# One step of a gated-linear-attention / gMLP decoder on one core: key halves joined in one row of matmuls, prompt states from fp32r parts, later state updates

## The chip, the cores and the metric

The kernel runs on one core of a Trainium2 chip. Its time is the device time of one execution in microseconds. A run's profile is the record of one execution by the hardware profiler; its span is the time from the first to the last instruction of the program. Engines are named as in the profile: PE multiplies matrices and PEld loads its weights, DVE and ACT do elementwise work, POOL and SP mostly start transfers here.

## The reference

The program computes one inference step of a decoder of two layers for two groups of tokens: a prompt of 256 new tokens, and 8 samples of 8 new tokens each. The model width is 2048.

Layer 0 mixes tokens by gated linear attention. Four heads have keys of 256 and values of 512. For each head a state S of 256 x 512 is carried along:

```
S_t = diag(a_t) S_{t-1} + k_t^T v_t          o_t = q_t S_t
o   = o * rsqrt(mean(o^2) + eps) * norm_g * silu(r)        then   o @ w_out
```

The prompt begins with S = 0 and returns its last state. Each sample brings a state of its own, and its eight tokens read that state and update it; the new state is an output too. q, k, v, r and a low-rank gate all come from one projection of x.

Layer 1 mixes tokens by a gMLP with a causal 128 x 128 matrix for each of eight groups. After each mixer comes `x = LayerNorm(alpha * x + mixer)`, then an MLP, `square(relu(x @ w1)) @ w2` with a hidden width of 8192, and again a LayerNorm of the sum. Everything is fp32.

## The kernel before

Activations lie with features on partitions and the 320 tokens (256 of the prompt, 64 of the samples) in the free dimension. The large products are done in three fp32r matmuls: both the weight and the activation are split into a high part (an fp32r cast) and a low part (the rest), and `mm3` adds low·high, high·low and high·high (L186 to L188). I call these the ordinary matmuls.

A unit of work is a weight tile of 512 rows by 256 columns. `unit` loads it from DRAM on SP's queue into `raw`, ACT casts it to the high part (L168) and DVE subtracts for the low part (L169). PE then does 2 x 4 x 3 = 24 matmuls over 320 columns. `group` walks the four units of a column block (`NU = 4`) and gives the finished PSUM tiles to an `evict` function. After each unit it calls `side`, which runs the next of a list of smaller steps: `Side` spreads its steps evenly over the units that are left, one or more to a unit, and `Spread` does the same with a fixed ratio. This order is that of emission. A scheduler then orders each engine's instructions by an estimated timeline, and may take a step earlier where its data are there.

In layer 0 each head takes 24 units: 8 for values (`project_v`), 8 for keys and queries (`project_kq`), 8 for the output gate r (`project_r`). The head's own attention is a list of steps (`Head.steps`) that runs beside `project_r` of the head and `project_v` of the next. In the last head there is no next `project_v`, and the list gets 10 units in place of 16. The steps that matter here:

- `split(n)`, n = 0 to 7: one quarter-head of two samples' states is brought into three bf16 parts (L632 to L635: cast, subtract, cast, subtract, each over 128 x 1024). The parts lie in four `sp` buffers, and each split starts the load of a later state on SP's queue.
- `sample_first` and `sample_group(kt)`: four samples at a time (`hd.g` is 0, then 1) multiply their queries with their states. `sample_first` is one fp32r matmul over 512 columns with the part within the eight tokens (L642). `sample_group(kt)` takes one half of the key dimension, kt = 0 or 1: three parts times four samples are 12 bf16 matmuls (L651), each with 32 columns of weights, that write the four quarters of one PSUM tile. `sample_out` evicts and transposes it.
- `prompt_scores`, `prompt_o(i)`: attention within the prompt, in fp32.
- `gather_k(q)`: transfers on POOL's queue (SP's in the last head) that finish the transposing of the prompt's decayed keys into `ktp`.
- `prompt_state(kt)`: the prompt's last state for one half of the key, `ktp` times the prompt's values in `va`, in fp32 (L604). It is evicted by ACT (L606) and stored.

In both MLPs the samples' states are updated beside the matmuls: `updates` yields a list of steps for 16 pairs of head and sample. A step `decay` scales a state on ACT, and eight steps `token` add one token's outer product each, two operations on DVE (L915). `paced` ties a step to the newest high part of a weight, so that it cannot run long before its place. `Spread` gives the 161 steps to 216 units. It starts with the third column block of the MLP's first product: the first two are done in raw form by `gemm_of`, while the LayerNorm is still being applied by `Norm.apply` (L853, L854, L856, L857, L859, the last of which writes the low part `yl`). The same `gemm_of` begins the gMLP layer's projection, with no updates beside it.

Of the kernel before, what the change touches and what calls it, by code (L numbers as in the profile page):

```python
# [8 lines left out]
F32 = mybir.dt.float32  # L9
F32R = mybir.dt.float32r  # L10
# [6 lines left out]
P = 128  # L17
D = 2048
KT = D // P
TP = 256  # L20
DB, DS = 8, 8
T = TP + DB * DS
TW = T + 2
H = 4
DK, DV = 256, 512
CH = 64
# [7 lines left out]
NU = KT // UK  # L34
# [62 lines left out]
def step_kernel(ctx: ExitStack, tc: tile.TileContext, A):  # L97
    nc = tc.nc
    uid = [0]

    def nm(s):
        uid[0] += 1
        return f"{s}_{uid[0]}"
# [23 lines left out]
    def gltile(n=512):  # L127
        return gl.tile([P, n], F32, tag="gl", name=nm("gl"), padded_shape=[P, 512])
# [20 lines left out]
    def col(c):  # L149
        return vec[:, c : c + 1]  # L150
# [88 lines left out]
    gp = gst.enter_context(tc.tile_pool(name="gp", bufs=1))  # L239
# [18 lines left out]
    def load_x(q):  # L258
        for i, raw in enumerate(x_in(q)):
            x_parts(slice(4 * q + 2 * i, 4 * q + 2 * i + 2), raw[:, :, 0:T])  # L260
# [10 lines left out]
    nc.vector.memset(smask[:, TP:T:DS], 0.0)  # L271

    W0, W1 = TP, TP - P
    mf = gp.tile([P, DV], F32, tag="kip", name="mf")[:, 0 : W0 + W1]
    nc.gpsimd.memset(mf, 1.0)
    for c0, w in ((0, W0), (W0, W1)):
        nc.gpsimd.affine_select(out=mf[:, c0 : c0 + w], in_=mf[:, c0 : c0 + w], compare_op=ALU.is_ge, fill=0.0,
# [21 lines left out]
    qm = gp.tile([P, 2, DB, 4, DS], BF16, tag="qm", name="qm")  # L299
# [48 lines left out]
    def pairs(t):  # L348

        return t[:].rearrange("p (a v f) -> p a v f", a=2, v=2)  # L350
# [12 lines left out]
    class Head:  # L363
# [5 lines left out]

        def tiles(hd):  # L370
            hd.qd = gp.tile([P, 2, T], F32, tag="qd", name=nm("qd"))
            hd.qx = gp.tile([P, 2, 5 * CH], F32, tag="qx", name=nm("qx"))
            hd.kip = gp.tile([P, 2, TP], F32, tag="kip", name=nm("kip"))
            hd.kte = gp.tile([P, 2, T], F32, tag="kte", name=nm("kte"))
            hd.kis = gp.tile([P, 2, DB, 2, DS], F32, tag="kis", name=nm("kis"))

            hd.ktp = gp.tile([P, 2, 2, P], F32, tag="ktp", name=nm("ktp"))
            hd.va = gp.tile([P, 2, 6, P], F32, tag="vtp", name=nm("va"))

        def vt_prompt(hd, vt, blk):  # L380
            return hd.va[:, vt // 2, vt % 2 * 2 + blk, :]

        def v_prompt(hd, blk):
            return hd.va[:, :, blk : blk + 3 : 2, :]

        def v_sample(hd):
            return hd.va[:, :, 4:6, :].bitcast(F32R)
# [211 lines left out]
        def prompt_state(hd, kt):  # L599
            if kt == 0:  # L600
                hd.S = g3.tile([P, 2, DV], F32, tag="st", name=nm("S"))
            pu = gltile()
            for blk in range(2):
                nc.tensor.matmul(pairs(pu), hd.ktp[:, kt, blk, :], hd.v_prompt(blk),  # L604
                                 start=(blk == 0), stop=(blk == 1))
            nc.scalar.copy(hd.S[:, kt, :], pu[:])  # L606
            if kt == 1:
                nc.gpsimd.dma_start(A["o_state_p"][hd.h].rearrange("(k p) v -> p k v", p=P), hd.S[:])
# [19 lines left out]
        def split(hd, n):  # L628

            s = hd.st.pop(n)  # L630
            hd.sp[n] = sp = g3.tile([P, 3, 2, DV], BF16, tag="sp", name=nm("sp"))
            nc.scalar.copy(sp[:, 0], s[:])  # L632
            nc.vector.tensor_sub(s[:], s[:], sp[:, 0])
            nc.scalar.copy(sp[:, 1], s[:])
            nc.vector.tensor_sub(sp[:, 2], s[:], sp[:, 1])  # L635
            if n + 3 < 8:
                hd.load(n + 3)
# [4 lines left out]
            nc.tensor.matmul(pairs(hd.po), scst[:, hd.g].rearrange("p j c t -> p (j c t)"), hd.v_sample(),  # L642
                             start=True, stop=False)

        def sample_group(hd, kt):

            n = 4 * hd.g + 2 * kt
            sp = [hd.sp.pop(n), hd.sp.pop(n + 1)]
            for c in (2, 1, 0):
                for j in range(4):  # L650
                    nc.tensor.matmul(hd.po[32 * j : 32 * (j + 1), :],  # L651
                                     qm[:, kt, 4 * hd.g + j].rearrange("p c t -> p (c t)"),
                                     sp[j // 2][:, c, j % 2, :], start=False, stop=(kt == 1 and c == 0))

        def sample_out(hd):

# [30 lines left out]
        def steps(hd):  # L687

            def split(n, also=lambda: None):
                return lambda: (also(), hd.split(n))  # L690

            yield hd.sample_scores
            yield hd.prompt_scores
            yield split(2, hd.sample_first)
            yield lambda: hd.prompt_o(0)
            yield lambda: (hd.sample_group(0), hd.gather_k(0))
            yield split(3, lambda: hd.prompt_o(1))
            yield split(4, lambda: hd.gather_k(1))
            yield lambda: (hd.sample_group(1), hd.gather_k(2))
            yield split(5, lambda: (hd.sample_out(), hd.gather_k(3)))  # L700
            yield split(6, hd.sample_first)
            yield lambda: hd.sample_group(0)
            yield split(7)
            yield lambda: hd.prompt_state(0)
            yield lambda: (hd.sample_group(1), hd.prompt_state(1))
            yield hd.sample_out
            yield hd.sums
            yield hd.weigh
            yield hd.finish
# [2 lines left out]
    warm_up()  # L712
    for h, hd in enumerate(hds):
        gates = [hd.gate_logits, hd.gate_sums, hd.gate_decays]
        if h == 0:

            side = Side([lambda: None, lambda: load_x(1), lambda: None, lambda: load_x(2), lambda: load_gates(),
                         lambda: load_x(3), low_gate, *gates], 4 * NU)
            hd.project_v(side)
            for step in (hd.begin_states, lambda: hd.split(0), lambda: hd.split(1)):  # L720
                side.steps.append(step)
            hd.project_kq(side)
        else:
            hd.project_v(side)
            hd.project_kq(Side([hd.begin_states, *gates, lambda: hd.split(0), lambda: hd.split(1)], 2 * NU))
        side = Side(hd.steps(), 2 * NU + (2 * NU if h < H - 1 else 2))
        hd.project_r(side)

# [150 lines left out]
    def updates(todo):  # L879
# [20 lines left out]
        def decay(h, b):  # L900
            st = cur[h, b]
            row(h, b, 0)
            row(h, b, 1)
            d = paced(dec_all[:, h, :, NCH + b])
            for kt in range(2):
                nc.scalar.activation(st[:, kt, :], st[:, kt, :], AF.Identity, scale=d[:, kt : kt + 1])
# [13 lines left out]
        begin(*todo[0])  # L920
        for i, (h, b) in enumerate(todo):
            if i == 0:
                yield lambda: None
                yield lambda: None
            yield lambda h=h, b=b: decay(h, b)
            for t in range(DS):
                yield lambda h=h, b=b, t=t: token(h, b, t)
                if t == 2 and i + 1 < len(todo):
                    yield lambda n=todo[i + 1]: begin(*n)
# [77 lines left out]
    def before(q):  # L1007
        if q == NU - 1:
            second_half()
        else:  # L1010
# [3 lines left out]
                         side=side, before=before)  # L1014
# [101 lines left out]
    for step in "n0 n2 m0 m1 n4 n6 m2 m3 m4 m5 n8 n10 m6 m7 m8 m9 n12 n14 m10 m11 m12 m13 m14 m15".split():  # L1116
        j = int(step[1:])
        steps.append((lambda j=j: mix2(j)) if step[0] == "n" else lambda j=j: mixed(j, *mix(j)))
    side = Side(steps, 6 * NU)
# [47 lines left out]
    for j in range(KT):  # L1167
        y, g, b = z[:, j, :], col(norm.vg + j), col(norm.vb + j)
# [4 lines left out]
        else:  # L1173
            if j not in ps:
                put_d(j)
            t = l2.tile([P, T], F32, tag="t", name=nm("t"), bufs=3)
# [70 lines left out]
```

## Time and profile before

| | us |
|---|---|
| median of 3 runs | 2664.23 |
| lowest and highest | 2663.86, 2664.64 |
| the profiled execution | 2665.18 |
| its span | 2663.4 |

| engine | busy us | share of the span |
|---|---|---|
| PE | 2651.9 | 100% |
| DVE | 1865.1 | 70% |
| ACT | 1330.6 | 50% |
| POOL | 383.0 | 14% |

The granted clock of PE is 1.0 throughout. Layer 0's four heads lie between about 5 and 405 us, the output projection follows, then the first MLP from about 517 us; the second MLP begins at about 1755 us. In the lists of groups a row shows the line, the engine, the operation, tiles written and read, shape and count, then the total busy time, the mean duration of one in ns, and the idle time before. In the timeline a row shows the start, the busy time, and how many instructions of the same kind were joined. A row of waits shows total, number and longest. A row of windows shows the stretch, its length, and for each engine (PE, PEld, DVE, ACT, POOL) its busy time and number of instructions; where it was asked for one line, only the engine of that line.

### The profile page before, as it was taken

The page shows a single profiled execution, that of the slowest core. Times are in us where ns is not written, and L with a number is a line of the kernel's source. Part 1 is how long each engine was busy: PE and PEld are TensorE (multiplying, and loading weights), DVE is VectorE, ACT ScalarE, POOL GpSimd, SP SyncE. Part 2 cuts the span into 40 slices and gives each one's busy share as a digit, 9 for nine tenths or more (in the row PEclk, how much of TensorE's full clock was granted, in tenths as well). Part 3 has the DMA queues.
Part 4 walks back from the last instruction along what each step waited for, and adds up shares of the span by engine and source line. Part 5 has one row for each costly group of instructions (what it writes and reads, how often), then busy time and mean ns, then how long its engine had stood idle before and what let it go on. Part 6 is the DMA issues. An engine that isn't in the chain of part 4 may idle for free.

```text
span 2663.4 us, 46772 instructions
## 1 busy us (share of the span) xinstructions
PE 2651.9 (100%) x18395; PEld 2625.8 (99%) x18395; DVE 1865.1 (70%) x2798; ACT 1330.6 (50%) x2290; POOL 383.0 (14%) x677
## 2 busy tenths in 40 slices
PE   9999999999999999999999999999999999999999
PEld 9999999999999999999999999999999999999998
DVE  7687686896667667667578765788666666666647
ACT  6575574574444345445346544466445444444434
POOL 4334320011111111111001041001111111111000
PEclk9999999999999999999999999999999999999999
DMA  8566566467767767677554454456767777676642
GB/s 262 164 214 197 155 207 235 149 187 227 225 218 219 223 214 230 213 226 216 177 153 159 151 167 149 150 153 215 231 212 225 216 218 228 213 229 212 198 151 95
DMA packets 163597, 524.88 MB, mean 197 GB/s; under 512 B 25520, under 2 KB 34608, under 8 KB 163376
## 3 DMA queue, kind: packets, MB, share of 16 engines
q1 hardware_dynamic: 121440, 408.08, 48.7%
q0 software_dynamic: 41392, 113.15, 14.5%
q8 instruction: 144, 2.36, 0.4%
q14 instruction: 77, 0.63, 0.1%
q10 hardware_dynamic: 544, 0.66, 0.1%
HBM read 493.48 MB, written 22.54 MB: 194 GB/s over the span
## 4 chain that ended last, share of the span: by engine, by line
PE 96%; DVE 2%; ACT 1%; DMA 1%; issue 0%; SPq 0%; ACTq 0%; DVEq 0%
PE mm L186 32%; PE mm L188 31%; PE mm L187 31%; PE gl L604 1%; DVE wl L169 1%; PE gl L651 0%; DMA st<-state 0%; PE gl L1096 0%; PE gl L588 0%; DMA raw<-gla_w_in 0%; ACT z L1180 0%; ACT wh L168 0%; DVE t L854 0%; DVE t L853 0%; DVE yl L859 0%
## 5 line engine op out<-in xcount | busy, mean ns | idle before, releaser
L169 DVE TENSOR_TENSOR wl<-raw,wh 128x1024 fp32r<-128x1024 f32 (+1 forms) x740 | 901.8, 1220 | 686.8 <-ACT wh L168 681.3
L168 ACT CAST wh<-raw 128x1024 fp32r<-128x1024 f32 (+1 forms) x740 | 771.7, 1044 | 1071.3 <-PE mm L188 937.0
L188 PE MATMUL mm<-yh,wh 128*128 128x320 f32 x2624 | 805.4, 307 | 0.0
L186 PE MATMUL mm<-yh,wl 128*128 128x320 f32 x2624 | 804.2, 308 | 0.0
L187 PE MATMUL mm<-yl,wh 128*128 128x320 f32 x2624 | 794.5, 303 | 2.3 <-DVE yl L859 2.3
L186 PE MATMUL mm<-hh,wl 128*128 128x320 f32 x2048 | 630.8, 308 | 0.0
L188 PE MATMUL mm<-hh,wh 128*128 128x320 f32 x2048 | 628.7, 307 | 0.0
L187 PE MATMUL mm<-hl,wh 128*128 128x320 f32 x2048 | 619.6, 303 | 0.0
L187 PEld LDWEIGHTS mm<-yl,wh 128*128 128x128 f32 x2624 | 492.5, 188 | 2.9 <-DVE yl L859 2.9
L186 PEld LDWEIGHTS mm<-yh,wl 128*128 128x128 f32 x2624 | 491.4, 188 | 0.0
L188 PEld LDWEIGHTS mm<-yh,wh 128*128 128x128 f32 x2624 | 490.8, 187 | 0.0
L187 PEld LDWEIGHTS mm<-hl,wh 128*128 128x128 f32 x2048 | 384.5, 188 | 0.0
L186 PEld LDWEIGHTS mm<-hh,wl 128*128 128x128 f32 x2048 | 384.4, 188 | 0.0
L188 PEld LDWEIGHTS mm<-hh,wh 128*128 128x128 f32 x2048 | 383.0, 187 | 0.0
L915 DVE SCALAR_TENSOR_TENSOR su<-vr,pace,su 128x512 f32<-128x512 f32 x512 | 363.8, 748 | 0.0
L886 POOL DMA_DIRECT2D vr<-v_dram x256 | 139.1, 544 | 1320.3 <-DVE su L915 1282.9
L186 PE MATMUL mm<-xh,wl 128*128 128x320 f32 x768 | 241.2, 316 | 1.5 <-DVE wl L169 1.0
L188 PE MATMUL mm<-xh,wh 128*128 128x320 f32 x768 | 236.7, 309 | 0.0
L187 PE MATMUL mm<-xl,wh 128*128 128x320 f32 x768 | 233.4, 304 | 0.0
L186 PEld LDWEIGHTS mm<-xh,wl 128*128 128x128 f32 x768 | 144.1, 188 | 8.6 <-issue 5.9
L187 PEld LDWEIGHTS mm<-xl,wh 128*128 128x128 f32 x768 | 144.2, 188 | 2.5 <-issue 1.7
L188 PEld LDWEIGHTS mm<-xh,wh 128*128 128x128 f32 x768 | 143.7, 187 | 0.2
(269 smaller groups left out, 2470.1 us busy)
## 6 DMA issues: line engine op xcount, KB each, us to landing
raw<-mlp_w SPq DMA_DIRECT2D x512, 512.0 KB, 4.0
vr<-v_dram POOLq DMA_DIRECT2D x256, 256.0 KB, 4.3
raw<-gla_w_in SPq DMA_DIRECT2D x94, 512.0 KB, 3.9
raw<-sg_w_in SPq DMA_DIRECT2D x64, 512.0 KB, 3.5
st<-state SPq DMA_DIRECT2D x32, 512.0 KB, 5.1
raw<-gla_w_out SPq DMA_DIRECT2D x32, 512.0 KB, 4.3
su<-state POOLq DMA_DIRECT2D x32, 512.0 KB, 6.8
o_state_s<-su POOLq DMA_DIRECT2D x32, 512.0 KB, 4.2
```

The costliest lines, as they stand in the source:

```text
L168: nc.scalar.copy(hi[:, ks, :], raw[:, ks, :])
L169: nc.vector.tensor_sub(lo[:, ks, :], raw[:, ks, :], hi[:, ks, :].bitcast(F32))
L186: nc.tensor.matmul(ps, wl[:, kk, s], x_h, start=first, stop=False)
L187: nc.tensor.matmul(ps, wh[:, kk, s], x_l, start=False, stop=False)
L188: nc.tensor.matmul(ps, wh[:, kk, s], x_h, start=False, stop=last)
L604: nc.tensor.matmul(pairs(pu), hd.ktp[:, kt, blk, :], hd.v_prompt(blk), start=(blk == 0), stop=(blk == 1))
L886: nc.gpsimd.dma_start(vt[:, 0:4, :], v_dram[h, b * DS + t].rearrange("(a f) -> a f", f=P).partition_broadcast(P))
L915: nc.vector.scalar_tensor_tensor(st[:, kt, :], v, k[:, kt : kt + 1], st[:, kt, :], op0=ALU.mult, op1=ALU.add)
```

## The change

Three things change.

Both halves of the key are done in one `sample_group`: 24 matmuls follow each other, and `sample_first` is called right before. Splits 0 to 3 are all listed beside `project_kq`, since the row needs all four. The list of steps has 16 entries where it had 18.

The prompt's states are made of fp32r parts: `split_kv` casts the prompt's values and keys to high parts and subtracts for the low ones, in place; `prompt_state` then adds low·high, high·low and high·high. The high parts need room, and take it from the tiles `qx`, `kip` and `kte`, which become slices of one tile `kqx`.

The list of updates begins with eight empty steps and not two.

```diff
-    mf = gp.tile([P, DV], F32, tag="kip", name="mf")[:, 0 : W0 + W1]
+    mf = gp.tile([P, 10 * CH + 2 * TP + 2 * T], F32, tag="kqx", name="mf")[:, 0 : W0 + W1]
...
             hd.qd = gp.tile([P, 2, T], F32, tag="qd", name=nm("qd"))
-            hd.qx = gp.tile([P, 2, 5 * CH], F32, tag="qx", name=nm("qx"))
-            hd.kip = gp.tile([P, 2, TP], F32, tag="kip", name=nm("kip"))
-            hd.kte = gp.tile([P, 2, T], F32, tag="kte", name=nm("kte"))
+            t = hd.scratch("kqx")
+            hd.qx, hd.kip, hd.kte = (v.rearrange("p (k t) -> p k t", k=2) for v in
+                                     (t[:, 0 : 10 * CH], t[:, 10 * CH : 10 * CH + 2 * TP], t[:, 10 * CH + 2 * TP :]))
...
+        def scratch(hd, name):
+            return gp.tile([P, 10 * CH + 2 * TP + 2 * T], F32, tag="kqx", name=nm(name))
...
-        def v_prompt(hd, blk):
-            return hd.va[:, :, blk : blk + 3 : 2, :]
+        def split_kv(hd):
+            t = hd.scratch("vk")
+            hd.vh = t[:, 0 : 8 * P].rearrange("p (a n f) -> p a n f", a=2, n=4).bitcast(F32R)
+            hd.kh = t[:, 8 * P : 12 * P].rearrange("p (k b f) -> p k b f", k=2, b=2).bitcast(F32R)
+            hd.vl, hd.kl = hd.va[:, :, 0:4, :], hd.ktp[:]
+            nc.scalar.copy(hd.vh, hd.vl)
+            nc.vector.tensor_sub(hd.vl.bitcast(F32R), hd.vl, hd.vh.bitcast(F32))
+            nc.scalar.copy(hd.kh, hd.kl)
+            nc.vector.tensor_sub(hd.kl.bitcast(F32R), hd.kl, hd.kh.bitcast(F32))
...
             pu = gltile()
-            for blk in range(2):
-                nc.tensor.matmul(pairs(pu), hd.ktp[:, kt, blk, :], hd.v_prompt(blk),
-                                 start=(blk == 0), stop=(blk == 1))
+            kh, kl, vh, vl = hd.kh, hd.kl.bitcast(F32R), hd.vh, hd.vl.bitcast(F32R)
+            for k, v in ((kl, vh), (kh, vl), (kh, vh)):
+                for blk in range(2):
+                    nc.tensor.matmul(pairs(pu), k[:, kt, blk, :], v[:, :, blk : blk + 3 : 2, :],
+                                     start=(k is kl and blk == 0), stop=(k is kh and v is vh and blk == 1))
...
-        def sample_group(hd, kt):
-            n = 4 * hd.g + 2 * kt
-            sp = [hd.sp.pop(n), hd.sp.pop(n + 1)]
-            for c in (2, 1, 0):
-                for j in range(4):
-                    nc.tensor.matmul(hd.po[32 * j : 32 * (j + 1), :],
...
+        def sample_group(hd):
+            for kt in range(2):
+                n = 4 * hd.g + 2 * kt
+                sp = [hd.sp.pop(n), hd.sp.pop(n + 1)]
+                for c in (2, 1, 0):
+                    for j in range(4):
+                        nc.tensor.matmul(hd.po[32 * j : 32 * (j + 1), :],
...
             yield hd.prompt_scores
-            yield split(2, hd.sample_first)
             yield lambda: hd.prompt_o(0)
-            yield lambda: (hd.sample_group(0), hd.gather_k(0))
-            yield split(3, lambda: hd.prompt_o(1))
-            yield split(4, lambda: hd.gather_k(1))
-            yield lambda: (hd.sample_group(1), hd.gather_k(2))
+            yield lambda: (hd.prompt_o(1), hd.gather_k(0))
+            yield lambda: (hd.sample_first(), hd.sample_group(), hd.gather_k(1))
+            yield split(4, lambda: hd.gather_k(2))
             yield split(5, lambda: (hd.sample_out(), hd.gather_k(3)))
-            yield split(6, hd.sample_first)
-            yield lambda: hd.sample_group(0)
+            yield split(6)
             yield split(7)
+            yield hd.split_kv
+            yield lambda: (hd.sample_first(), hd.sample_group())
             yield lambda: hd.prompt_state(0)
-            yield lambda: (hd.sample_group(1), hd.prompt_state(1))
-            yield hd.sample_out
+            yield lambda: (hd.prompt_state(1), hd.sample_out())
...
+        states = [lambda n=n: hd.split(n) for n in range(4)]
...
-            for step in (hd.begin_states, lambda: hd.split(0), lambda: hd.split(1)):
-                side.steps.append(step)
+            side.steps += [hd.begin_states, *states]
...
-            hd.project_kq(Side([hd.begin_states, *gates, lambda: hd.split(0), lambda: hd.split(1)], 2 * NU))
+            hd.project_kq(Side([hd.begin_states, *gates, *states], 2 * NU))
...
             if i == 0:
-                yield lambda: None
-                yield lambda: None
+                for _ in range(8):
+                    yield lambda: None
```

More of the change, by code (lines that the diff above doesn't have):

```diff
@@ L643, in sample_first @@
                              start=True, stop=False)
-        def sample_group(hd, kt):
-            n = 4 * hd.g + 2 * kt
-            sp = [hd.sp.pop(n), hd.sp.pop(n + 1)]
-            for c in (2, 1, 0):
-                for j in range(4):
-                    nc.tensor.matmul(hd.po[32 * j : 32 * (j + 1), :],
-                                     qm[:, kt, 4 * hd.g + j].rearrange("p c t -> p (c t)"),
-                                     sp[j // 2][:, c, j % 2, :], start=False, stop=(kt == 1 and c == 0))
+        def sample_group(hd):
[5 more added lines that the diff above has]
+                        nc.tensor.matmul(hd.po[32 * j : 32 * (j + 1), :],
+                                         qm[:, kt, 4 * hd.g + j].rearrange("p c t -> p (c t)"),
+                                         sp[j // 2][:, c, j % 2, :], start=False, stop=(kt == 1 and c == 0))
         def sample_out(hd):
```

## The prediction

> **What bounds the kernel now.** I read the head of the page and the list of PE's waits first, then the timeline of PE around each stretch that the change touches, then windows by stage for the engines beside it.
>
> ```profile
> span 2663.4 us, 46772 instructions
> PE 2651.9 (100%) x18395; PEld 2625.8 (99%) x18395; DVE 1865.1 (70%) x2798; ACT 1330.6 (50%) x2290; POOL 383.0 (14%) x677
> ```
>
> ```profile
> PE mm L187 <- DVE yl L859: 2.3, 2, 1.5
> ...
> PE mm L186 <- DVE wl L169: 1.0, 1, 1.0
> PE mm L186 <- ACT oh L734: 0.4, 1, 0.4
> PE mm L186 <- DVE kis L448: 0.3, 1, 0.3
> ```
>
> PE is never long without work: of 2663.4 us it lacks 11.5. So the time is the number of matmuls times what each takes on PE, plus a few stalls; a change of another engine's work counts only where PE waits for it. Because the recorded ends of matmuls overlap, I price everything by starts: the distance from the last ordinary matmul before an insertion to the second one after it, less two ordinary steps.
>
> ```profile
> 95.29 0.31 PE L188 MATMUL mm<-xh,wh 128*128 128x320 f32 x1
> 95.53 0.83 PE L651 MATMUL gl<-sp,qm 128*32 128x512 bf16 x12
> 96.29 0.41 PE L186 MATMUL mm<-xh,wl 128*128 128x320 f32 x1
> 96.54 0.31 PE L187 MATMUL mm<-xl,wh 128*128 128x320 f32 x1
> ...
> 103.67 0.31 PE L188 MATMUL mm<-xh,wh 128*128 128x320 f32 x1
> 103.82 0.40 PE L642 MATMUL gl<-va,scst 128*128 128x512 f32 x1
> 104.05 0.31 PE L186 MATMUL mm<-xh,wl 128*128 128x320 f32 x1
> 104.20 0.31 PE L187 MATMUL mm<-xl,wh 128*128 128x320 f32 x1
> ...
> 114.73 0.30 PE L187 MATMUL mm<-xl,wh 128*128 128x320 f32 x1
> ...
> 115.31 0.31 PE L188 MATMUL mm<-xh,wh 128*128 128x320 f32 x1
> 115.45 1.88 PE L604 MATMUL gl<-va,ktp 128*128 128x512 f32 x4
> 116.77 0.71 PE L186 MATMUL mm<-xh,wl 128*128 128x320 f32 x1
> 117.32 0.31 PE L187 MATMUL mm<-xl,wh 128*128 128x320 f32 x1
> ```
>
> An ordinary step is (115.31 − 114.73) / 4 = 0.145. Twelve matmuls of L651 cost 96.54 − 95.29 − 0.29 = 0.96. One fp32r matmul over 512 columns (L642) costs 104.20 − 103.67 − 0.29 = 0.24. The four records of L604, which are two fp32 matmuls over 512 columns in two records each, cost 117.32 − 115.31 − 0.29 = 1.72, or 0.43 a record.
>
> **Part one: 24 matmuls in one row.** Nothing is added or removed: sample_group's two calls, one for each half of the key, now stand back to back.
>
> ```profile
> L604 PE MATMUL gl<-va,ktp 128*128 128x512 f32 x32 | 15.4, 605 | 0.0
> L651 PE MATMUL gl<-sp,qm 128*32 128x512 bf16 x192 | 13.3, 383 | 0.0
> ```
>
> The 192 matmuls are 16 insertions of twelve, and they become 8 of 24. Twelve matmuls are three rounds, because four of them stand side by side on 32 columns each. A round streams 512 columns: 0.215 if it goes like half a record of L604, 0.24 if like L642. Three rounds are 0.645 to 0.72, so 0.24 to 0.315 of the 0.96 is the way into the narrow shape and out of it (the ordinary matmul before L651 is followed after 0.24 and not 0.145, the one after it after 0.25). Each merged pair pays this once less. I take 0.315, because the insertions of L604 show the pass without any change of shape: 8 × 0.315 = **−2.5**, with 1.9 as the small end; zero is a rival below. sample_first moves next to the row at the same 0.24, and prompt_o and the transposes keep their price.
>
> The states must be in bf16 parts earlier: splits 0 to 3 are all emitted in the key and query stretch, where before only 0 and 1 were. But the scheduler already takes them there.
>
> ```profile
> 236.00:264.00 28.00, 4.16 (x4) 1.00 0.81 244
> ```
>
> This is L632, the first cast of a split, in the window of head 2's keys and queries: four of them, so no work moves into that stretch. Splits 4 to 7 now wait for the whole row, about two units later than the first pair did, and have six units, some 6 × 24 × 0.145 = 21 us, until the second row needs them, for 4 × 2 × 1.22 = 9.8 us of DVE. In the last head it is three units, and there I allow up to 1 us of stall in the range.
>
> ```profile
> st<-state SPq DMA_DIRECT2D x32, 512.0 KB, 5.1
> ```
>
> The state loads on SP's queue follow the splits one for one in the same order; gather_k's DMAs go out on POOL's queue (SP's in the last head) at most one unit earlier. I cost both at nothing, since no transfer is in the list of PE's waits; uncovered, one late load would be one landing, 5.1 us.
>
> **Part two: the prompt's states from fp32r parts.** Per head it adds split_kv, two casts on ACT and two subtractions on DVE over 1024 and 512 columns, and turns four fp32 matmuls into twelve in fp32r.
>
> ```profile
> L633 DVE TENSOR_TENSOR st<-st,sp 128x1024 f32<-128x1024 f32 x32 | 38.6, 1217 | 5.2 <-ACT sp L632 5.1
> ```
>
> ```profile
> 264.00:300.00 36.00, 35.66 (x271) 33.32 (x270) 28.02 (x53) 23.02 (x34) 8.68 (x16) 1.00 0.56 174
> 363.00:405.00 42.00, 41.57 (x306) 35.74 (x306) 27.29 (x49) 24.58 (x38) 0.72 (x1) 1.00 0.50 160
> ```
>
> DVE gets 1.22 + 0.61 = 1.8 us a head and ACT about 1.6; in these windows, the output-gate projection of heads 2 and 3, DVE (third figure) has 8 and 14.7 us free and ACT (fourth) 13 and 17. That hides it. Uncovered it would cost its 1.8 us a head. The new wait is that ACT's cast of ktp stands behind the gathers, with the casts of the weights queued after it; but split_kv stands three units after the last gather, one in the last head, and PE waits for L169 only once, at the start.
>
> On PE six fp32r matmuls replace four records per half of the key. At 0.215 each they cost 1.29, at 0.24 1.44; saved is 0.28 to 0.43. I take 0.225, 1.35, because L642's 0.24 holds its change to and from 320 columns as well: 8 × (1.72 − 1.35) = **−3.0**, from −2.2 to −3.4.
>
> ```profile
> L187 PEld LDWEIGHTS mm<-hl,wh 128*128 128x128 f32 x2048 | 384.5, 188 | 0.0
> ```
>
> A weight load takes 0.188 and an ordinary step 0.145, so loads run beside matmuls here.
>
> The Trainium skill, "TensorE: Matmul & The Clock Gate", Part 3, The mechanism, speaks against this: weights load during a running matmul only when the two use different row groups, and all twelve use all of them. By that rule each would pay its weight load in the open. The trace disagrees, at 0.145 a step.
>
> **Part three: the state updates start later.** Each MLP's Spread has eight empty steps instead of two: 167 steps over 216 units, so the first decay runs at unit 11 of the spread and not 3. That is 8 × 24 × 0.145 = 28 us, with 4% more steps per unit after it, on a DVE that is busy 70% of the time.
>
> ```profile
> 553.34 0.45 PE L186 MATMUL mm<-yh,wl 128*128 128x320 f32 x2
> 554.59 0.41 PE L187 MATMUL mm<-yl,wh 128*128 128x320 f32 x1 [0.80 <-DVE yl L859]
> 554.85 0.31 PE L188 MATMUL mm<-yh,wh 128*128 128x320 f32 x1
> ...
> 1791.93 0.45 PE L186 MATMUL mm<-yh,wl 128*128 128x320 f32 x2
> 1793.91 0.41 PE L187 MATMUL mm<-yl,wh 128*128 128x320 f32 x1 [1.53 <-DVE yl L859]
> 1794.16 0.31 PE L188 MATMUL mm<-yh,wh 128*128 128x320 f32 x1
> ```
>
> ```profile
> 546.12 1.42 DVE L915 SCALAR_TENSOR_TENSOR su<-vr,pace,su 128x512 f32<-128x512 f32 x2
> ...
> 550.65 1.43 DVE L915 SCALAR_TENSOR_TENSOR su<-vr,pace,su 128x512 f32<-128x512 f32 x2
> ...
> 554.04 0.50 DVE L859 TENSOR_TENSOR yl<-z,yh 128x320 fp32r<-128x320 f32 x1
> ```
>
> Both waits for yl stand at the second column group of an MLP. The loss is 554.85 − 553.34 − 3 × 0.145 = 1.08 and 1794.16 − 1791.93 − 0.435 = 1.80, together 2.9. Ahead of the late yl DVE does four updates, 1.42 + 1.43 = 2.85 us, more than either loss; 28 us later they stand behind all of the norm. The third norm of this form, before the gMLP layer, has no updates and is not in the list of waits. What is late next is the norm's own chain, which in the second MLP runs later than in the first by about the difference of the two losses, 0.7 us. So I take **−2.5**, between −1.8 and −2.9.
>
> **The sum.** −2.5 − 3.0 − 2.5 = −8.0. The profiled execution took 2665.18, its span of 2663.4 and 1.8 around it; it goes to 2657.2. The median of the runs is 0.95 below it: 2664.23 − 8.0 = **2656.2**. With all large ends and the kis wait gone (0.3, and 0.1 for the slower step after it) it is −9.2, 2655.0; with all small ends and 1 us of stall in the last head −4.9, 2659.3.
>
> **Rivals.**
> Row without gain: the way in and out is paid in every round of four, and a row of 24 costs 1.92. For it: three rounds of 0.24 plus gaps would also fit 0.96. Against: the slow steps stand at the two edges. −5.5, 2658.7.
>
> The yl wait stays: the norm's chain is late by itself, or other work takes the updates' place. For it: the scheduler places work by its own estimate, not by these times. Against: the third norm. −5.5, 2658.7.
>
> Weights in the open, the slower side: in the rows of six, each fp32r matmul waits for its own weights. Each then takes 0.24 + 0.188 = 0.43, six 2.57 against 1.72, so +0.85 × 8 = +6.8; with the other two parts +1.8, 2666.0. It decides from 0.29 a matmul on, where six equal the four records. Against it stand the 2048 loads quoted above, hidden in steps of 0.145. The skill page named above is its rule.
>
> DVE overrun before the key eviction: the kis wait shows no room there, and two more splits would really enter.
>
> ```profile
> 236.00:264.00 28.00, 28.00 (x195) 28.00 (x195) 25.48 (x43) 23.86 (x33) 13.30 (x24) 1.00 0.81 244
> 335.00:363.00 28.00, 28.00 (x196) 28.00 (x195) 26.34 (x48) 24.59 (x35) 13.31 (x24) 1.00 0.87 262
> ```
>
> DVE has 2.5 and 1.7 us free; two splits are 4 × 1.22 = 4.9, so 2.8 a head are over, 11.2 in four heads: +3.2, 2667.4. Against it is the count of four casts already there.
>
> **How the numbers follow.** Forecast 0.72; row without gain 0.06; yl wait stays 0.09; weights in the open 0.05; DVE overrun 0.05; 0.03 for what I don't see. A measurement of this kernel tells about 0.2%, 5.3 us, from no change, so faster means below 2658.9. The forecast lies there nearly whole (0.70), the two cases at 2658.7 somewhat over half (0.09): faster 0.79. The two slow cases lie mostly within 5.3 us above: slower 0.04, same 0.17. The range goes from 2653.8, a little past the large ends, to 2659.6, past the two half-gains and the small ends.
>
> **What would show it.** Right: one L651 group x24, eight times, 1.6 us from the step before to the step after; six fp32r matmuls in 1.35; no wait for yl above 0.7; the first L915 some 28 us after its old place; four casts L632 in the key stretch, as now. Wrong: a fp32r step above 0.29, a wait of PE for a split, for the parts of ktp or va, or a longer one for kis.

## The result, and the profile after

| | before | after |
|---|---|---|
| median of 21 runs each, us | 2663.96 | 2659.87 |
| the profiled execution, us | 2665.18 | 2659.83 |
| its span, us | 2663.4 | 2658.1 |

After against before is 0.9984, with an interval of 0.9977 to 0.9991: 4.1 us faster, where 8.0 was forecast. The profiled execution of before was 1.2 us above its median and that of after was not, so the two traces differ by more, 5.3 us, than the runs do. One of the 21 runs of after, at a granted clock of 0.559, took 4365.18 us; the medians include it, the ratio leaves it out.

The head of the page of after, and its list of PE's waits (total, number, longest):

```profile
span 2658.1 us, 46888 instructions
PE 2647.0 (100%) x18411; PEld 2628.0 (99%) x18411; DVE 1870.6 (70%) x2806; ACT 1337.2 (50%) x2298; POOL 382.9 (14%) x677
```

```profile
PE mm L186 <- DVE kis L460: 2.2, 3, 0.9
...
PE mm L187 <- DVE ol L748: 0.3, 1, 0.3
```

DVE and ACT are busy some 6 us longer, the work of `split_kv`; PE is busy all the time, as before. The wait for `yl`, 2.3 us before, is gone. The wait for `kis`, 0.3 us once before, is now 2.2 us in three places: once in each of heads 1, 2 and 3. `kis` is the last of the three products with which DVE empties the first key tile from PSUM, and PE wants that tile back for its next column block.

Now the places that the prediction priced. First the row and the states in the timeline of PE of after (start, busy time, instruction, count), in head 0 and, from 388 us on, the last head's second row:

```profile
112.63 0.31 PE L188 MATMUL mm<-xh,wh 128*128 128x320 f32 x1
112.77 0.40 PE L656 MATMUL gl<-va,scst 128*128 128x512 f32 x1
113.10 1.48 PE L666 MATMUL gl<-sp,qm 128*32 128x512 bf16 x24
...
114.76 0.31 PE L187 MATMUL mm<-xl,wh 128*128 128x320 f32 x1
...
117.95 0.31 PE L188 MATMUL mm<-xh,wh 128*128 128x320 f32 x1
118.10 0.62 PE L618 MATMUL gl<-vk,ktp 128*128 128x512 f32 x2
118.56 0.63 PE L618 MATMUL gl<-va,vk 128*128 128x512 f32 x2
119.03 0.62 PE L618 MATMUL gl<-vk 128*128 128x512 f32 x2
...
119.63 0.31 PE L187 MATMUL mm<-xl,wh 128*128 128x320 f32 x1
...
388.29 0.83 PE L666 MATMUL gl<-sp,qm 128*32 128x512 bf16 x12
...
390.64 0.39 PE L666 MATMUL gl<-sp,qm 128*32 128x512 bf16 x2
...
392.75 0.82 PE L666 MATMUL gl<-sp,qm 128*32 128x512 bf16 x10
```

Priced by starts, the row with its first matmul costs 114.76 − 112.63 − 0.29 = 1.84. Without L656's 0.24 that is 1.60 against 2 × 0.96 before. The six fp32r matmuls cost 119.63 − 117.95 − 0.29 = 1.39, or 0.232 each. Seven of the eight rows are whole. So one way into the narrow shape and out of it costs 2 × 0.96 − 1.60 = 0.32, and a round of four (1.60 − 0.96) / 3 = 0.21. The last head's second row is not whole: the scheduler put one of the `prompt_state` insertions after its first twelve matmuls and ordinary matmuls after two more. The pieces together cost 0.82 more than a whole row. Two ways in and out and the round that the second break cuts in two would be 0.85.

Then the second MLP at the matmuls where before waited longest for `yl`, and the first MLP's first state update on DVE:

```profile
1787.96 0.45 PE L186 MATMUL mm<-yh,wl 128*128 128x320 f32 x2
1788.25 0.30 PE L187 MATMUL mm<-yl,wh 128*128 128x320 f32 x1
1788.39 0.31 PE L188 MATMUL mm<-yh,wh 128*128 128x320 f32 x1
```

```profile
567.35 1.42 DVE L928 SCALAR_TENSOR_TENSOR su<-vr,pace,su 128x512 f32<-128x512 f32 x2
```

No wait is left: L187 starts 0.29 after the two L186, where it took 1.98 before. The first update starts 21 us after its old place at 546.12, and 24 us later in its MLP, whose first ordinary matmul starts 2.9 us earlier in after.

Last, the key tile in head 2, on PE and on DVE:

```profile
260.61 0.31 PE L188 MATMUL mm<-xh,wh 128*128 128x320 f32 x1
261.79 0.42 PE L186 MATMUL mm<-xh,wl 128*128 128x320 f32 x1 [0.87 <-DVE kis L460]
262.04 0.31 PE L187 MATMUL mm<-xl,wh 128*128 128x320 f32 x1
```

```profile
255.75 1.23 DVE L649 TENSOR_TENSOR sp<-st,sp 128x1024 bf16<-128x1024 f32 x1 [0.37 <-ACT sp L648]
...
258.38 1.22 DVE L649 TENSOR_TENSOR sp<-st,sp 128x1024 bf16<-128x1024 f32 x1
259.58 1.22 DVE L169 TENSOR_TENSOR wl<-raw,wh 128x1024 fp32r<-128x1024 f32 x1
260.72 0.48 DVE L458 TENSOR_TENSOR kqx<-mm,ee 128x320 f32<-128x320 f32 x1
...
261.45 0.28 DVE L460 TENSOR_TENSOR kis<-mm,ei 128x128 f32<-128x128 f32 x1
```

PE is held up for 262.04 − 260.61 − 0.29 = 1.14, which is 0.27 more than the wait as listed. Three such waits are 2.2 + 3 × 0.27 = 3.0 us. Before there was one, at 0.6 by the same count. On DVE the last subtractions (L649) of two splits start 2.6 us apart, and the second ends 1.1 us ahead of the key products. In before the second one ended about as close, 1.2 us ahead, but the first started 5.5 us before it. That both now come so late is what the experiments had to explain.

### The profile page after: what moved, and what is told of

It is laid out like the page before. It is cut to its first block, busy times and chain, and to the rows that moved or that the text cites. A ratio compares the mean times of both kernels' runs of the same rounds, so it can differ in the third digit from the quotient of the medians.

```text
span 2658.1 us, 46888 instructions
## 1 busy us (share of the span) xinstructions
PE 2647.0 (100%) x18411; PEld 2628.0 (99%) x18411; DVE 1870.6 (70%) x2806; ACT 1337.2 (50%) x2298; POOL 382.9 (14%) x677
## 4 chain that ended last, share of the span: by engine, by line
PE 95%; ACT 2%; DMA 1%; DVE 1%; issue 1%; POOL 0%; SPq 0%; ACTq 0%; DVEq 0%
PE mm L186 31%; PE mm L188 31%; PE mm L187 30%; DMA st<-state 1%; ACT wh L168 0%; PE gl L666 0%; PE gl L618 0%; DVE wl L169 0%; PE gl L1109 0%; PE gl L600 0%; DMA raw<-gla_w_in 0%; ACT z L1193 0%; ACT sp L646 0%; ACT sp L648 0%; DMA va<-blk 0%
## 5 line engine op out<-in xcount | busy, mean ns | idle before, releaser
L186 PE MATMUL mm<-yh,wl 128*128 128x320 f32 x2624 | 802.8, 308 | 0.0
L187 PE MATMUL mm<-yl,wh 128*128 128x320 f32 x2624 | 794.5, 303 | 0.0
L186 PE MATMUL mm<-hh,wl 128*128 128x320 f32 x2048 | 630.8, 308 | 0.0
L187 PE MATMUL mm<-hl,wh 128*128 128x320 f32 x2048 | 619.6, 303 | 0.0
L187 PEld LDWEIGHTS mm<-yl,wh 128*128 128x128 f32 x2624 | 492.6, 188 | 0.0
L186 PEld LDWEIGHTS mm<-yh,wl 128*128 128x128 f32 x2624 | 491.0, 188 | 0.0
L187 PEld LDWEIGHTS mm<-hl,wh 128*128 128x128 f32 x2048 | 384.5, 188 | 0.0
L186 PEld LDWEIGHTS mm<-hh,wl 128*128 128x128 f32 x2048 | 384.4, 188 | 0.0
L186 PE MATMUL mm<-xh,wl 128*128 128x320 f32 x768 | 239.9, 313 | 2.8 <-DVE kis L460 2.2
L187 PE MATMUL mm<-xl,wh 128*128 128x320 f32 x768 | 233.4, 304 | 0.0
L186 PEld LDWEIGHTS mm<-xh,wl 128*128 128x128 f32 x768 | 144.0, 188 | 8.2 <-issue 3.2
L187 PEld LDWEIGHTS mm<-xl,wh 128*128 128x128 f32 x768 | 144.3, 188 | 0.9 <-DVE xl L256 0.4
```

The costliest lines, as they stand in the source:

```text
L186: nc.tensor.matmul(ps, wl[:, kk, s], x_h, start=first, stop=False)
L187: nc.tensor.matmul(ps, wh[:, kk, s], x_l, start=False, stop=False)
```

## The experiments

First each part ran alone, to see whether the gains add up, and beside them a kernel that takes the new wait away by other means.

### One part at a time, and the keys apart from the queries

**Part one alone.** Before, with `sample_group` and the lists of after; the list of steps has 15 entries, since `split_kv` is not there.

```diff
+            yield lambda: (hd.sample_first(), hd.sample_group(), hd.gather_k(1))
...
             yield split(7)
+            yield lambda: (hd.sample_first(), hd.sample_group())
             yield lambda: hd.prompt_state(0)
-            yield lambda: (hd.sample_group(1), hd.prompt_state(1))
-            yield hd.sample_out
+            yield lambda: (hd.prompt_state(1), hd.sample_out())
```

> The kernel before with part one alone: the row of 24 with its new list of steps, splits 0 to 3 listed beside the keys and queries; the states stay fp32, the updates start early. Theory A (the new list of steps itself delays the eviction of the keys and breaks the last row): 7 whole rows save 0.31 each, but the waits of PE for kis grow from 0.3 to about 2.2 us as in the changed kernel, so the time is within 1 us of before, and both waits for yl stay (2.3). Theory B (the delay of the eviction comes from the merged tile and the new work of part two): kis stays near 0.3 and the time is 2.5 to 3.4 us below before.

Measured: 2661.58 against 2664.01, ratio 0.999 [0.9981, 0.9999]: −2.4 us. Its list of waits has no `kis`, so theory A fails as to the waits. The last row is broken here too, into 2, 10, 2 and 10 matmuls, which cost 2.95 where a whole row costs 1.60.

**Part two alone.** Before, with `split_kv` as a step of its own and the fp32r `prompt_state`, the old order of the rest (19 entries) and two empty steps.

```diff
             yield split(7)
+            yield hd.split_kv
             yield lambda: hd.prompt_state(0)
```

> The kernel before with part two alone: split_kv after split 7, six fp32r matmuls a half, qx, kip and kte in one tile. Theory A: 8 x 0.34 = 2.7 us faster, kis waits near 0.3 us as before. Theory B: the six matmuls save the same 2.7 but the waits for kis grow by about 2 us, so 0.5 to 1 us faster.

Measured: 2662.32 against 2664.01, ratio 0.9995 [0.9986, 1.0003]: −1.7 us, with the interval reaching past no change. Its runs spread from 2661.63 to 2664.39. A `kis` wait of 0.5 us stands once in its list.

**Part three alone.** Before, with

```diff
-                yield lambda: None
-                yield lambda: None
+                for _ in range(8):
+                    yield lambda: None
```

> The kernel before with part three alone: eight empty steps ahead of the updates. If the two waits for yl are made by the four updates ahead of it and by nothing else: no wait for yl, and 2.9 us faster (0.97 + 0.11 and 1.69 + 0.11 by starts of matmuls). If the norm's own chain is late: a wait of up to 0.7 us stays in the second MLP and it is about 2.2 us faster.

Measured: 2661.53 against 2664.01, ratio 0.999 [0.9982, 0.9999]: −2.5 us, no wait for `yl` and none for `kis`.

**After, with keys and queries in column blocks of their own.** PE then no longer comes back for the first key tile while DVE is busy with it; the same products are done in another order.

```diff
-                if n == 0:
+                if n == 2:
...
-            group(w_in, 0, (C_K + h * DK, C_Q + h * DK), xh, xl, ev, side)
+            for n0, c in ((0, C_K), (2, C_Q)):
+                group(w_in, 0, (c + h * DK,), xh, xl, lambda n, ps, n0=n0: ev(n0 + n, ps), side)
```

> The changed kernel, but keys and queries in column groups of their own, so that the keys are evicted four units before the output gate's first matmul needs their PSUM tile. If the 2.2 us of waits for kis are the eviction standing behind other work of DVE after the joint group: they go, and the time is about 2.5 us below the changed kernel, 2657.4. Rival (DVE is full in that stretch, so the lateness only moves): the wait turns up at the weights' low parts or at the queries' eviction, and the time stays at 2659.9.

Measured: 2657.41 against 2664.01, ratio 0.9975 [0.9965, 0.9984]: 2.5 us faster than after, and no wait for `kis`.

What follows: the parts alone give 2.4 + 1.7 + 2.5 = 6.6 us, together they give 4.1. The 2.5 that are missing are what taking the `kis` waits away gives back, and about what those waits grew by in the trace, 3.0 − 0.6 = 2.4. Part two's 1.7 is the loose figure among them, since its runs spread over 2.8 us. So the loss looks like an interaction: neither the row nor the fp32r states bring the three waits about alone.

### Which interaction

Two accounts were left. Either the work that each part puts on DVE adds up in the key stretch (the rival "DVE overrun"), or the number of steps does it. The list of part one has 15 entries and that of after 16, over the same 16 units. At 16 entries `prompt_state(1)` is the 13th and runs in the 13th unit; at 15 it is the 12th. In before it was the 14th of 18, and since the first two units took two steps each, it ran in the 12th as well. So in after it comes one unit later, and with it the store of `S`, the head's last state, which it issues on POOL's queue.

**After, with `split_kv` in one step with `split(7)`.** 15 entries, all work as in after.

```diff
-            yield split(7)
-            yield hd.split_kv
+            yield lambda: (hd.split(7), hd.split_kv())
```

> The changed kernel, with split_kv in the step of split 7 instead of one of its own: the same work, but 15 steps, so that each head's last step (finish, four multiplications on DVE) ends one unit before the next head's keys and queries and not with them. Theory S (the place of these last steps makes the eviction of the keys late): the waits for kis fall from 2.2 to below 0.5 and the time by about 2 us, to 2657.8. Theory W (split_kv's work and the merged tile themselves): the waits stay at about 2.2 and the time at 2659.9.

Measured: 2656.25 against 2664.17, ratio 0.997 [0.9958, 0.9981]: −7.9 us. No wait for `kis`.

**Part one alone, with an empty sixteenth step** where `split_kv` would stand. It computes what part one computes.

```diff
             yield split(7)
+            yield lambda: None
             yield lambda: (hd.sample_first(), hd.sample_group())
```

> Part one alone, with an empty step where the changed kernel has split_kv: no work is added, but the list has 16 steps as there. Theory S: waits for kis appear, 1.5 to 2.2 us in all, and the time rises from part one's 2661.6 to about 2663.5. Theory W: no wait for kis, and the time stays at 2661.6.

Measured: 2664.99 against 2664.17, ratio 1.0003 [0.9995, 1.0012]: 3.4 us slower than part one alone, which took no such wait. From its list of PE's waits:

```profile
PE mm L186 <- DVE kis L448: 2.4, 3, 1.2
```

An empty step brings all three waits, which by starts cost 3.2 us, so no added work of `split_kv` is needed for them; the number of steps is enough. Why it is, these two runs leave open: theory S puts it down to the last step, `finish`, but the store of `S` moves by the same unit.

**After, with splits 2 and 3 listed beside `project_r` again.**

```diff
-        states = [lambda n=n: hd.split(n) for n in range(4)]
+        states = [lambda n=n: hd.split(n) for n in range(2)]
...
-            yield lambda: hd.prompt_o(0)
-            yield lambda: (hd.prompt_o(1), hd.gather_k(0))
+            yield split(2, lambda: hd.prompt_o(0))
+            yield split(3, lambda: (hd.prompt_o(1), hd.gather_k(0)))
```

> The changed kernel, with splits 2 and 3 listed beside prompt_o again, not beside the keys and queries. If their place in the list matters to the stretch of the keys: less DVE work there, 2 x 2.44 = 4.9 us per head, and no wait for kis, 2657.6. If the scheduler takes them as early as their buffers allow, as before: four first casts of a split in that stretch as now, waits for kis of 1.5 to 2.5, and 2659.9 within 0.7.

Measured: 2659.83 against 2664.17, ratio 0.9983 [0.9974, 0.9992], the time of after. Its windows over ACT's cast at L646 (stretch, length, busy, count) in the key stretch of head 2:

```profile
233.00:261.00 28.00, 4.16 (x4) 1.00 0.82 254
```

The `kis` waits stand in it as in after, 2.4 us in three places. Four splits run in that stretch wherever they are listed, as before the change too. This refutes the overrun in the form that the prediction gave it, with two more splits entering.

**Keys apart, and the last head's row behind both `prompt_state` steps,** for the broken row.

```diff
-            yield lambda: (hd.sample_first(), hd.sample_group())
-            yield lambda: hd.prompt_state(0)
-            yield lambda: (hd.prompt_state(1), hd.sample_out())
+            row = lambda: (hd.sample_first(), hd.sample_group())
+            if hd.h < H - 1:
+                yield row
...
+            else:
+                yield lambda: hd.prompt_state(0)
+                yield lambda: hd.prompt_state(1)
+                yield row
+                yield hd.sample_out
```

> Keys and queries in groups of their own, and in the last head the second row comes after both prompt states instead of before them, so that splits 4 to 7 have one more unit. If the last row was broken into 12, 2 and 10 matmuls because its last parts were not ready: it stands as one row of 24 and the time falls by 0.6 to 1.0 from keys apart alone, to 2656.6. Rival (another matter of order): the row is still broken, or the steps after it come later, and the time stays at 2657.4.

Measured: 2656.30 against 2664.17, ratio 0.9969 [0.9958, 0.9981]; 1.1 us below the kernel with keys apart, which was measured on another chip, and the row is whole.

### How one unit of a store becomes three waits of PE

The queues of after at the end of head 1. First ACT, then POOL's and SP's issues:

```profile
221.49 0.59 ACT L620 COPY S<-gl 128x512 f32<-128x512 f32 x1 [0.29 <-PE gl L618]
```

```profile
221.29 6.35 POOL L361 DMA_DIRECT2D va<-blk  x11 [0.92 <-PE gl L618]
227.63 0.72 POOL L622 DMA_DIRECT2D o_state_p<-S  x1
228.34 2.84 POOL L361 DMA_DIRECT2D va<-blk  x5
```

```profile
227.80 0.33 SPq L162 DMA_DIRECT2D raw<-gla_w_in  x1
228.17 0.95 SPq L640 DMA_DIRECT2D st<-state  x2
231.81 9.83 SPq L162 DMA_DIRECT2D raw<-gla_w_in  x3
241.69 4.28 SPq L640 DMA_DIRECT2D st<-state  x3
```

`S` is complete on ACT at 222.1, but its store goes out at 227.63, behind eleven gathers of the next head's values. `S` lies in the ring `st` of the loaded states (`hd.S = g3.tile(..., tag="st")`), which has four buffers. In the order of the kernel the next tiles of this ring are the next head's second value block and its first three states. Handed out in turn, the buffer of `S` goes to the fourth tile after it, which is the third state: its load needs the buffer that this store reads. On SP that load no longer follows the first two; it stands behind three weight loads, at 241.69. In before the store stood behind five of the gathers, and the three loads went out with one weight load between:

```profile
223.86 2.84 POOL L361 DMA_DIRECT2D va<-blk  x5
226.70 0.72 POOL L608 DMA_DIRECT2D o_state_p<-S  x1
```

```profile
232.27 1.58 SPq L626 DMA_DIRECT2D st<-state  x2
235.21 0.34 SPq L162 DMA_DIRECT2D raw<-gla_w_in  x1
235.59 0.66 SPq L626 DMA_DIRECT2D st<-state  x1
```

In after, splits 2 and 3 thus get their data late and end up right ahead of the key products, as the rows of DVE above show. With `split_kv` joined to `split(7)` the store, the loads and DVE stand like this, one fence for each engine:

```profile
218.11 0.72 POOL L622 DMA_DIRECT2D o_state_p<-S  x1 [0.39 <-ACT o_all L680]
...
221.00 1.71 POOL L361 DMA_DIRECT2D va<-blk  x3
```

```profile
228.04 1.79 SPq L640 DMA_DIRECT2D st<-state  x3
```

```profile
254.00 1.22 DVE L649 TENSOR_TENSOR sp<-st,sp 128x1024 bf16<-128x1024 f32 x1
...
258.06 0.48 DVE L458 TENSOR_TENSOR kqx<-mm,ee 128x320 f32<-128x320 f32 x1
```

The store is ahead of the gathers, the three loads go together, and the last L649 ends 2.8 us before the key products begin, where in after it was 1.1. The kernel that puts this chain to the test moves nothing but the store:

**After, with the store on ACT's queue.**

```diff
-                nc.gpsimd.dma_start(A["o_state_p"][hd.h].rearrange("(k p) v -> p k v", p=P), hd.S[:])
+                nc.scalar.dma_start(A["o_state_p"][hd.h].rearrange("(k p) v -> p k v", p=P), hd.S[:])
```

> The changed kernel, with the store of the prompt's state started from ACT's queue instead of POOL's; the list keeps its 16 steps. Theory Q (the store stands on POOL behind the next head's value gathers, so the tile st comes free late, the third state load of the next head is started 9 us into its keys and queries, and the splits that wait for it crowd DVE ahead of the eviction of the keys): the third load starts before the keys, the waits for kis fall from 2.2 below 0.5, and the time by 2 to 3.5 us, to 2656.3 to 2657.8. Rival (the number of steps matters in another way than by this store): the waits stay at about 2.2 and the time at 2659.9.

Measured: 2656.66 against 2663.95, ratio 0.9972 [0.996, 0.9983]: 3.2 us faster than after, at the same 16 steps. Its state loads on SP, and its longest wait of PE:

```profile
227.29 2.23 SPq L640 DMA_DIRECT2D st<-state  x3
```

```profile
PE gl L177 <- DVE ones L136: 1.1, 1, 1.1
```

The three loads are together again and `kis` is gone from the list. So it is the store's place on POOL's queue that brought the waits. It is not the last step, `finish`: it has the same place in the list as in after. The traces of the other kernels fit, and so does head 0, which has no store ahead of it and no wait. The first three figures of a row are those of head 2 (the store is that of head 1), and the waits, by starts, are summed over all heads:

| kernel | gathers right ahead of the store | weight loads between the first and the third state load | last two L649 apart, us | waits for `kis`, us |
|---|---|---|---|---|
| before (L635 there) | 5 | 1 | 5.5 | 0.6 |
| part one alone | 0 | 0 | 7.3 | 0 |
| part one, 16 steps | 11 | 3 | 2.6 | 3.2 |
| part two alone | 0 | 0 | 10.3 | 0.8 |
| part three alone (L635) | 5 | 1 | 5.5 | 0 |
| after | 11 | 3 | 2.6 | 3.0 |
| after, splits 2 and 3 late | 11 | 3 | 2.6 | 3.3 |
| after, joined step | 0 | 0 | 8.9 | 0 |
| after, store on ACT | on ACT | 0 | 5.6 | 0 |

The three waits stand where the store is behind eleven gathers, and nowhere else. Part two alone shows that one smaller wait can come without this chain; where its 0.8 comes from was not found. The kernel with keys apart, not in the table, has the store and the loads of after; there PE comes back for the tile later, and finds it empty. One link is not seen in any of them: each engine's order is fixed before the program runs, by the scheduler's estimate, and no trace shows how that estimate set the three weight loads ahead of the state load. That they follow the store is shown. The landing of the store held the load up for a part of that time at most: these stores land 5.9 us after their issue in the median of after, here at about 233.5, and the load goes out 8.2 us later.

### The two remaining kernels

**15 steps and the row behind the states in the last head,** the two repairs together.

```diff
-            yield split(7)
-            yield hd.split_kv
...
+            yield lambda: (hd.split(7), hd.split_kv())
+            row = lambda: (hd.sample_first(), hd.sample_group())
+            if hd.h < H - 1:
+                yield row
...
+            else:
+                yield lambda: hd.prompt_state(0)
+                yield lambda: hd.prompt_state(1)
+                yield row
+                yield hd.sample_out
```

> split_kv in the step of split 7, and in the last head the second row after both prompt states. If the two losses are apart from each other: 2656.25 less about 1.0 for the last row, 2655.3, no wait for kis and eight whole rows of 24. Rival: with 15 steps the last row's broken form cost nothing that is left to win, 2656.2.

Measured: 2655.84 against 2663.95, ratio 0.9969 [0.9957, 0.9981]: −8.1 us, the fastest here. Its last row and one of its waits:

```profile
387.38 1.48 PE L666 MATMUL gl<-sp,qm 128*32 128x512 bf16 x24
```

```profile
PE mm L187 <- DVE ol L754: 0.6, 1, 0.6
```

The row is whole, but over the kernel with the joined step alone, measured on another chip, this gains 0.2 us by the differences to before, inside the spread of the runs. There the last row lies in four pieces that cost 3.1, and the whole one costs 1.6. Of these 1.5 us the trace has 0.9 come back, by starts, as the wait for `ol`, the low part of the last head's output, which the later row delays.

**After, with four empty steps in each MLP,** for how much of the delay is needed.

```diff
-                for _ in range(8):
+                for _ in range(4):
```

> The changed kernel with four empty steps ahead of the updates instead of eight: the first decay at unit 6 of the spread, 10 us after its place in the kernel before and not 28. If it is enough that the four updates ahead of the late yl go behind it, which took 2.85 us: no wait for yl, and the time of the changed kernel. If the updates then still stand ahead of later parts of the norm: a wait for yl of 0.5 to 1.5 us in at least the second MLP.

Measured: 2660.16 in one run. Its waits show no `yl` either. By this one trace, two more empty steps than before would have done.

## Why the prediction was right or wrong

The sign was right, and each of the three gains is there, though the rows gave less than was forecast. The forecast was low by 3.7 us mainly because it counted nothing for a loss that came with part one and part two together.

| term of the sum, us | forecast | by the trace |
|---|---|---|
| rows of 24 | −2.5 | −1.7 |
| fp32r states | −3.0 | −2.7 |
| later updates | −2.5 | −2.9 |
| `kis` | 0 | +2.4 |
| `prompt_scores`, `sample_scores` | 0 | −0.9 |

The rest of the trace's 5.3 us: the output projection's wait for `ol` (+0.3), an end 0.4 later and a start 0.5 earlier, where before's profiled execution had its wait of 1.0 for `wl`; some 0.3 are not put down to anything.

**The row of 24.** Right in price: 1.60 against the forecast's 1.605 (2 × 0.96 − 0.315). Both edges cost 0.32 together, once for each row and not once for each round of four, so "row without gain" is refuted. Seven whole rows give −2.2. The eighth is the place where the prediction allowed up to 1 us in the last head; not a stall came there but a broken row, at 0.82. Part one alone came out at −2.4, so near the −2.5, by luck: in its trace the rows give only −1.2, since its last one lies in four pieces; the scores give −1.2 more and the missing `kis` wait −0.6.

**The fp32r states.** Right in kind, 0.04 us short for each six: 1.39 and not 1.35, that is 8 × 0.34 = −2.7 (1.73 less 1.39, the means of the insertions that stand alone). "Weights in the open" is refuted: 0.232 a matmul lies under the 0.29 from which that rival decides. The Trainium skill's page "TensorE: Matmul & The Clock Gate" states two things here. The list of what overlaps in its Part 3, The mechanism, lets a weight load run beside a matmul only in another row group; its Part 2, Step-by-step: what each phase is for, also lets it run ahead where it goes to a background buffer of weights, and so does the opening of that Part 3. The rows speak against the first and fit the second: loads of 0.188 and six matmuls on all rows at 0.232 each leave no room for a load in the open. That such a buffer does it, no trace shows. Alone, part two brought 1.7 us by its median and not 2.7. Its runs spread over more than the missing 1.0, and what makes them differ was not found; its one `kis` wait of 0.5 is a part of it at most.

**The later updates.** Right, and a little better, −2.9 in the trace: both `yl` waits are gone whole, so the residual of up to 0.7 us that the prediction left for the norm's own chain was not there. The updates came 21 us later (24 in their MLP) and not 28, which made no difference, since with four empty steps no wait for `yl` stood either.

**The step that failed** is in part one: "The state loads on SP's queue follow the splits one for one in the same order; gather_k's DMAs go out on POOL's queue (SP's in the last head) at most one unit earlier. I cost both at nothing". The step that was moved past a queue was another one. Part two's entry in the list and part one's shorter list put `prompt_state(1)` one unit later, and the prediction followed its matmuls but not its store: the store went behind eleven gathers on POOL's queue where it had stood behind five, its buffer is in the ring of the state loads, and the loads did not follow each other any more. In place of nothing this cost 2.4 us in the trace; the kernel with nothing but the store moved to ACT's queue takes 3.2 us less, 2656.66, and that is 0.5 from the forecast. Bounded by "one landing, 5.1 us" if uncovered, the item was there in kind; its price was taken as zero because no transfer stood among PE's waits. None stands there now either: the wait is filed under `kis` on DVE, three links away.

**The rival "DVE overrun before the key eviction"** had the place right and both the mechanism and the price wrong. Four splits run in the key stretch before and after, so no work was added; the last two run closer together at its end. It cost 0.6 to 1.2 us in each of three heads and nothing in head 0, not 2.8 in each of four.

**What was not foreseen on the good side:** the score matmuls now stand in fewer pieces. In head 0 of before and of after, from the last ordinary matmul ahead of the last piece:

```profile
74.25 0.30 PE L186 MATMUL mm<-xh,wl 128*128 128x320 f32 x1
74.48 0.38 PE L573 MATMUL gl<-qx,kte 128*64 128x192 f32 x1
...
75.43 0.31 PE L188 MATMUL mm<-xh,wh 128*128 128x320 f32 x1
```

```profile
74.78 0.31 PE L188 MATMUL mm<-xh,wh 128*128 128x320 f32 x1
75.01 0.34 PE L579 MATMUL gl<-qd,kqx 128*64 128x64 f32 x4
...
76.76 0.30 PE L187 MATMUL mm<-xl,wh 128*128 128x320 f32 x1
```

In after `prompt_scores` is one piece of 76.76 − 74.78 − 0.29 = 1.69. In before its second half alone, a piece of its own, is 75.43 − 74.25 − 0.29 = 0.89, and its first half, joined with the end of `sample_scores`, 1.0. Both kinds of scores together fell from 2.76 to 2.15 in head 0 and from 2.44 to 2.15 in heads 1 and 2, and rose to 2.73 in the last: −0.9. Why the scheduler cut them so was not tried. It is luck that this gain about covers the 0.8 of the broken row; neither was in the sum.

## What to carry to other kernels

When a step is moved by even one place in a list, list every transfer it issues, the queue it issues them on, what stands on that queue around the new place, and which ring the transfer's buffer belongs to; a store that is issued late can put off a load that needs its buffer. That the list of PE's waits names no transfer is no proof that transfers are free: look for the engine work that a transfer releases, and how close that work stands to an eviction that PE needs. Try the parts alone and together before trusting their sum: here one step more or less in a list decided over 3 us of 8.

## What the hardware showed that was not expected

An issue of a transfer waited for its place on the engine's queue though its data were there: the store's data were complete at 222.1 and it was issued at 227.63, right at the end of eleven gathers that took POOL 6.35 us. The Trainium skill's page "Perfetto Trace Analysis", Tensor Engine Instruction (MATMUL, LD_WEIGHTS), states that GpSimd, like DVE and ACT, keeps strict order; this trace agrees, with those 6.3 us between the gathers' start and the store.

The way into and out of the 32-column shape costs 0.32 us here, whether one, three or six rounds lie between: 0.96 for three rounds and 1.60 for six make a round (1.60 − 0.96) / 3 = 0.213 and the rest 0.32, and a piece of two matmuls, one round, cost 0.52 in part one alone, where that sum gives 0.53. An fp32r matmul over the same 512 columns takes 0.232, not much more, where an fp32 one took two records of 0.43: three fp32r products cost less than one in fp32.
